# Twelve gate columns of an input projection: one split weight tile, or an fp32 product in four column groups

## The chip, the cores and the metric

The kernel runs on one core of a Trainium2 chip. The metric is the device time of one execution in microseconds. Before the change the median of three runs is 1077.58 us (1074.95 to 1078.34).

## What is computed

One inference step of a two-layer decoder, for 256 prompt tokens and 8 single-token samples, 264 columns in all, 1024 features wide. Each layer projects the normalised input with one wide matrix, feeds the pieces to four recurrent mixers (RWKV7, HGRN2, Mamba2, mLSTM), projects back, and adds cross attention over a memory and a feed-forward block:

```python
proj = rmsnorm(x, lp['norm_mix_g']) @ lp['w_in']
p_r, p_h, p_s, p_m = jnp.split(proj, GROUP_SPLITS, axis=-1)
...
x = x + mixed @ lp['w_out']
x = x + cross_attend(rmsnorm(x, lp['norm_x_g']), mem_k, mem_v, lp['xattn_wq'], lp['xattn_wo'])
hf = rmsnorm(x, lp['norm_ff_g']) @ lp['ff_w1']
x = x + jnp.square(jax.nn.relu(hf)) @ lp['ff_w2']
```

Twelve columns of `w_in` matter here. Four are Mamba2's step sizes (`dt_pre`), four the mLSTM's input gates and four its forget gates, one column per head. Everything is fp32.

## The kernel before

The activations stand transposed: `xT[k]` is feature block k (128 features) by 264 columns, k = 0 to 7. A dense product takes an fp32 weight tile `raw` of 1024 x 128 (512 KB, one DMA on SP), which ACT casts in two halves to the reduced type fp32r (`wh`, line 231) and DVE subtracts (`wl`, line 93, the rest). Its input is split in the same way, `xh` and `xl`, with the norm's gain folded in. For each of the eight blocks `dense` issues three products, wh·xh, wh·xl and wl·xh (lines 295, 296, 297), into one accumulator: 24 products a tile. The norm's factor `rstd` is multiplied in when DVE reads the accumulator. `raw` has four buffers, `wh` and `wl` three halves each.

A layer begins with eight such tiles of `w_in`, in the order 6, 2, 3, 0, 1, 4, 5, 7. The first seven are the RWKV columns. Tile 7 holds the twelve gate columns, at columns 0 to 3, 32 to 35 and 64 to 67, and zeros elsewhere; `small_rows` (line 858) turns its result `sy` into the step sizes and gates. Then three generators (RWKV, HGRN2 with mLSTM after it, Mamba2) are interleaved with the remaining `w_in` tiles and the memory's keys and values as filling work. The order of each engine's list is made by a scheduler from the order in which the program issues the work and from priorities (`later` lowers one). Each engine takes its list strictly in order.

`C(name)` is a piece of a table of constants that is loaded after the first weight tiles. Names in the rows: `LT`, `lw` are the low-rank stage of the RWKV mixer (line 410), `KV`, `qd`, `pd` with line 1365 are the cached part of the cross attention. Line 1365 issues fp32 products with 8 columns each, at accumulator partitions 0, 32, 64 and 96:

```python
for i in range(2):
    for hh in range(2):
        for a in range(2):
            b, g = b0 + a, (hh * 2 + a) * 32
            PE.matmul(ps[g:g + 8, :], lhsT=lhs[:, hh, i, b * 8:b * 8 + 8], rhs=kv[a][hh][:, i],
                      start=b < 2 and i == 0, stop=b >= NB - 2 and i == 1)
```

Of the kernel before, what the change touches and what calls it, by code (L numbers as in the profile page):

```python
# [8 lines left out]
F32 = mybir.dt.float32  # L9
# [6 lines left out]
DEPTH, DM, TP, NB, NT = 2, 1024, 256, 8, 264  # L16
KT = DM // 128
# [12 lines left out]
C_RW, C_HG, C_SS, C_ML = 0, 896, 1920, 2948  # L30


def build_consts():
    p = np.arange(128)
    cols, off, n = [], {}, 0

    def add(name, a):
        nonlocal n
        a = np.asarray(a, np.float32).reshape(128, -1)
        off[name] = (n, a.shape[1])  # L40
        n += a.shape[1]
        cols.append(a)

    add("ident", np.eye(128))
    add("blk64", (p[:, None] // 64) == (p[None] // 64))
    t64 = np.arange(64)
    s64 = (p % 64)[:, None]
    add("msi", np.concatenate([t64[None] > s64, t64[None] >= s64], 1))
    add("mh", np.stack([(p // 32) % 2 == 0, (p // 32) % 2 == 1], 1))
    t32 = np.arange(32)  # L50
    s32 = (p % 32)[:, None]
    add("id32", t32[None] == s32)
    for w in (1, 2, 4, 8, 16):
        add(f"inv{w}", ((t32[None] // w) % 2 == 1) & (s32 // w == t32[None] // w - 1))
    add("h0", t64[None] == s64)
    for w in (1, 4, 16):
        for d in (1, 2, 3):
            t = (np.arange(0, 64, 4 * w)[:, None] + np.arange(d * w, 4 * w)).reshape(-1)
            add(f"h{w}{d}", s64 // w == t[None] // w - d)
    add("mneg", np.where(p[None] >= p[:, None], 0.0, -1e30))  # L60
    add("pick", (p % 32)[:, None] == np.arange(4)[None])
    add("eye8", np.broadcast_to(np.eye(8), (128, 8, 8)))
    add("nsc", np.where(p < 32, -2.0, np.where(p < 64, 0.0, -1.0)))
    add("sgn", np.where(p >= 64, -1.0, 1.0))
    return np.ascontiguousarray(np.concatenate(cols, 1)), off
# [5 lines left out]
def body(tc, A, O, depth=DEPTH):  # L71
    nc = tc.nc
    V, S, P, PE = nc.vector, nc.scalar, nc.gpsimd, nc.tensor
# [10 lines left out]
    spool = pool("sm", 1)  # L84
# [10 lines left out]
    def mul(out, a, b):  # L95
        return tt(out, a, b, ALU.mult)
# [77 lines left out]
    xT = [xTt[:, k] for k in range(KT)]  # L174
# [1301 lines left out]
    def layer(l):  # L1476
# [34 lines left out]
            else:  # L1511
                small.append(small_rows(l, pv, ps, rstd))

        for m in (6, 2, 3, 0, 1, 4, 5, 7):
            tag = {3: "pa", 0: "pb"}.get(m, "pd") if l == 0 else "pd"
            dense([A["w_in"][l, m]], xh, xl, ev, m, ready if m == 6 else (), tag)
            if l == 0 and m == 2:
                derive(0)
            if l == 0 and m == 0:
                nc.sync.dma_start(cst, A["consts"])  # L1520
                for i in range(1, depth):
                    nc.sync.dma_start(pvt[i][:, 0:NPV], A["pv"][i])
        if l == 0 and depth > 1:
            derive(1)
        if l == 0:
# [6 lines left out]
        def proj(m0, name, order=(0, 1, 2, 3)):  # L1532
            out = [T("J", [128, 2, NT], f"{name}{i}") for i in range(4)]

            def go():
                for i in order:
                    for c in range(2):
                        dense([A["w_in"][l, m0 + 2 * i + c]], xh, xl, lambda m, ps: mul(out[i][:, m], ps, rstd), c)
                        yield
            return out, go()  # L1540

# [2 lines left out]
        def conv():  # L1544
            smp.append(tiny([128, 6, NB, 4], "smp"))
            nc.sync.dma_start(smp[0], A["conv"][l])
            for g in range(3):
                t = T("J", [128, 2, 259], "CAT")
                V.memset(t[:, :, 0:3], 0.0)

                def ev_c(m, ps, t=t):
                    mul(t[:, m, 3:259], ps[:, 0:TP], rstd[:, 0:TP])
                    mul(smp[0][:, 2 * g + m, :, 3], ps[:, TP:NT], rstd[:, TP:NT])
                for c in range(2):
                    dense([A["w_in"][l, 18 + 2 * g + c]], xh, xl, ev_c, c)
                    yield
                CAT.append(t)
            Z.append(T("J", [128, 2, NT], "Z"))
            for c in range(2):
                dense([A["w_in"][l, 16 + c]], xh, xl, lambda m, ps: mul(Z[0][:, m], ps, rstd), c)  # L1560
                yield

        PH, d_hg = proj(8, "PH", (1, 0, 2, 3))
# [143 lines left out]
def pack(x):  # L1707

    x = {k: np.asarray(v) for k, v in x.items()}
    A = {"consts": CONSTS}  # L1710
    t = np.concatenate([x["x_prompt"][0], x["x_sample"][:, 0]], 0)
    A["x"] = t.T.reshape(KT, 128, NT).transpose(1, 0, 2)
    A["mem"] = x["mem_prompt"][0].T.reshape(KT, 128, TP).transpose(1, 0, 2)

    def tiles(w):
        d, k, n = w.shape
        w = w.reshape(d, k // 1024, 8, 128, n // 128, 128).transpose(0, 4, 1, 3, 2, 5)
        return w if k > 1024 else w[:, :, 0]
    w = x["w_in"]
    sm = np.zeros((DEPTH, DM, 128), w.dtype)  # L1720
    sm[:, :, 0:4] = w[:, :, C_ML - 4:C_ML]
    sm[:, :, 32:36] = w[:, :, C_ML + 768:C_ML + 772]
    sm[:, :, 64:68] = w[:, :, C_ML + 772:C_ML + 776]
    A["w_in"] = tiles(np.concatenate([w[:, :, 0:896], sm, w[:, :, 896:C_ML - 4], w[:, :, C_ML:C_ML + 768],
                                      w[:, :, C_ML + 776:]], 2))
    for nm, k in (("wq", "xattn_wq"), ("wk", "xattn_wk"), ("ff1", "ff_w1"), ("ff2", "ff_w2")):
        A[nm] = tiles(x[k])

    w = x["xattn_wv"].reshape(DEPTH, 2, 4, 128, 4, 256).transpose(0, 4, 1, 3, 2, 5)
    A["wv"] = w.reshape(DEPTH, 4, 2, 128, 8, 128)  # L1730

    def halves(w):
        w = w.reshape(DEPTH, 2, 4, 128, 4, 2, 128).transpose(0, 1, 4, 3, 5, 2, 6)
        return w.reshape(DEPTH, 2, 4, 128, 8, 128)
    A["w_out"] = halves(x["w_out"].reshape(DEPTH, 4, 256, DM)[:, list(ORDER)])
    A["wo"] = halves(x["xattn_wo"])
    pv = np.zeros((DEPTH, 128, NPV), np.float32)
    for l in range(DEPTH):
        for nm, (o, n) in POFF.items():
            if nm in ("lb0", "lb1"):  # L1740
                v = x["hgrn_lb_logits"][int(nm[2])]
            elif nm == "final_norm_g":
                v = x[nm]
            elif nm == "D":
                v = np.repeat(x["ssm_D"][l], 64)
            elif nm in ("sbias", "alog"):
                v = np.zeros(128, np.float32)
                if nm == "sbias":
                    v[0:4], v[32:36], v[64:68] = x["ssm_dt_bias"][l], x["mlstm_i_bias"][l], x["mlstm_f_bias"][l]
                else:  # L1750
                    v[0:4] = x["ssm_A_log"][l]
            else:
                v = x[nm][l]
            pv[l, :, o:o + n] = v.reshape(n, 128).T
    A["pv"] = pv
    A["lora"] = np.concatenate([x["rwkv_w_up"], x["rwkv_a_up"], x["rwkv_g_up"]], 1)
    A["shift"] = x["state_rwkv_shift"].reshape(DEPTH, NB, 7, 128).transpose(0, 3, 2, 1)
    c = np.zeros((DEPTH, 128, 6, NB, 4), np.float32)
    c[..., 0:3] = x["state_ssm_conv"].reshape(DEPTH, NB, 3, 6, 128).transpose(0, 4, 3, 1, 2)
    A["conv"] = c  # L1760

    def quarters(s):
        return s.reshape(DEPTH, NB, 4, 4, 16, -1).transpose(0, 3, 1, 2, 4, 5).reshape(DEPTH, 128, 16, -1)
    A["wkv"], A["hgrn"] = quarters(x["state_rwkv_wkv"]), quarters(x["state_hgrn"])
    A["ssm"], A["mC"] = quarters(x["state_ssm"]), quarters(x["state_mlstm_C"])
    keyed = lambda s: s.reshape(DEPTH, NB, 2, 2, 64, 64).transpose(0, 3, 4, 2, 1, 5).reshape(DEPTH, 128, 16, 64)
    A["wkvT"], A["mCT"] = (keyed(x[k].swapaxes(3, 4)) for k in ("state_rwkv_wkv", "state_mlstm_C"))
    A["hgrnT"] = keyed(x["state_hgrn"])
    A["ssmT"] = x["state_ssm"].reshape(DEPTH, NB, 2, 2, 64, 128).transpose(0, 5, 2, 1, 3, 4).reshape(DEPTH, 128, 16, 128)
    A["mnT"] = x["state_mlstm_n"].reshape(DEPTH, NB, 2, 128).transpose(0, 3, 2, 1)  # L1770
    rep = lambda s: np.concatenate([s.reshape(DEPTH, 32, -1)] * 4, 1)
    A["mn"], A["mm"] = rep(x["state_mlstm_n"]), x["state_mlstm_m"].transpose(0, 2, 1)
    A["ck"] = x["cache_mem_k"].reshape(DEPTH, NB, 256, 4, 2, 128).transpose(0, 1, 3, 5, 4, 2)
    A["cv"] = x["cache_mem_v"].reshape(DEPTH, NB, 2, 128, 4, 256).transpose(0, 1, 4, 3, 2, 5)
    return {k: np.ascontiguousarray(v) for k, v in A.items()}
# [36 lines left out]
```

## Time and profile before

| | before |
|---|---|
| median of three runs | 1077.58 us (1074.95 to 1078.34) |
| the profiled execution | 1075.53 us |
| its span, first to last instruction | 1073.8 us |
| PE busy | 1047.8 us, 98% |
| DVE busy | 806.4 us, 75% |
| ACT busy | 630.9 us, 59% |
| mean granted TensorE clock | 0.979 |

PE is TensorE's products, PEld its weight loads, DVE VectorE, ACT ScalarE, SP the engine that issues the DMAs. Products overlap in the array, so a product's duration is longer than the distance from its start to the next start; the distance is what it takes of PE's time. An fp32 product leaves two records.

### The profile page before, as it was taken

The numbers are of one execution on the slowest core, as the hardware profiler recorded it, in microseconds if no ns is written. First come the engines' busy times: TensorE is split into PE (matmuls) and PEld (weight loads), VectorE is DVE, ScalarE is ACT, GpSimd is POOL, SyncE is SP. The second block draws the span as 40 slices with busy tenths as digits, with TensorE's granted clock in tenths as the row PEclk, the third lists the DMA queues.
The fourth block names the chain that finished last, engine by engine and source line by source line (L and its number), as shares of the span: only waits on it lengthen the run. The fifth ranks groups of instructions, "written<-read, shape, count | busy, mean of one in ns | idle before, by whom it ended". The sixth has DMA issues, their size and how long they took to land.

```text
span 1073.8 us, 26237 instructions
## 1 busy us (share of the span) xinstructions
PE 1047.8 (98%) x10334; PEld 979.0 (91%) x10334; DVE 806.4 (75%) x1846; ACT 630.9 (59%) x1352; POOL 51.7 (5%) x75
## 2 busy tenths in 40 slices
PE   8998999999999999999999999999999999999996
PEld 8997898889878999999999989888997789999996
DVE  6889785678778987755669887855886799775544
ACT  5965464467555676645569455735674466775543
POOL 2000000001001100000010000000020020000000
PEclk8999998999999999999999999989999999999999
DMA  7743456469894685555554454645978758555552
GB/s 247 235 144 102 116 150 205 149 225 329 268 361 164 232 284 183 182 178 178 186 178 158 129 142 125 192 151 167 307 251 303 277 179 293 185 177 186 180 177 80
DMA packets 81579, 213.44 MB, mean 199 GB/s; under 512 B 16432, under 2 KB 19120, under 8 KB 81456
## 3 DMA queue, kind: packets, MB, share of 16 engines
q1 hardware_dynamic: 81456, 211.77, 61.0%
q8 instruction: 81, 1.33, 0.5%
q14 instruction: 42, 0.34, 0.1%
HBM read 195.86 MB, written 15.87 MB: 197 GB/s over the span
## 4 chain that ended last, share of the span: by engine, by line
PE 90%; DVE 6%; ACT 1%; DMA 1%; issue 0%; POOL 0%; SPq 0%; DVEq 0%; ACTq 0%
PE pd L295 20%; PE pd L297 20%; PE pd L296 20%; PE pm L1365 3%; PE pd L308 3%; PE pd L309 2%; PE pd L310 2%; PE pd L1318 1%; PE pd L1319 1%; PE pm L1427 1%; PE pd L1320 1%; DVE wl L93 1%; PE pm L1452 1%; PE pm L345 1%; PE pm L150 1%; PE pm L941 1%
## 5 line engine op out<-in xcount | busy, mean ns | idle before, releaser
L231 ACT CAST wh<-raw 128x512 fp32r<-128x512 f32 x544 | 335.5, 619 | 281.2 <-PE pd L296 228.6
L93 DVE TENSOR_TENSOR wl<-raw,wh 128x512 fp32r<-128x512 f32 x544 | 378.2, 699 | 153.8 <-ACT wh L231 142.6
L295 PE MATMUL pd<-xh,wh 128*128 128x264 f32 x1136 | 332.1, 292 | 0.4 <-ACT wh L231 0.4
L297 PE MATMUL pd<-xh,wl 128*128 128x264 f32 x1136 | 328.4, 289 | 2.9 <-DVE wl L93 2.9
L296 PE MATMUL pd<-xl,wh 128*128 128x264 f32 x1136 | 327.1, 288 | 2.4 <-DVE xl L111 2.4
L295 PEld LDWEIGHTS pd<-xh,wh 128*128 128x128 f32 x1136 | 217.1, 191 | 7.1 <-issue 2.8
L297 PEld LDWEIGHTS pd<-xh,wl 128*128 128x128 f32 x1136 | 217.8, 192 | 5.3 <-DVE wl L93 4.5
L296 PEld LDWEIGHTS pd<-xl,wh 128*128 128x128 f32 x1136 | 217.1, 191 | 3.3 <-DVE xl L111 3.0
L295 PE MATMUL pd<-hid,wh 128*128 128x264 f32 x512 | 146.0, 285 | 0.0
L297 PE MATMUL pd<-hid,wl 128*128 128x264 f32 x512 | 145.7, 285 | 0.0
L296 PE MATMUL pd<-hid,wh 128*128 128x264 f32 x512 | 145.5, 284 | 0.0
L296 PEld LDWEIGHTS pd<-hid,wh 128*128 128x128 f32 x512 | 96.6, 189 | 0.0
L297 PEld LDWEIGHTS pd<-hid,wl 128*128 128x128 f32 x512 | 96.4, 188 | 0.0
L295 PEld LDWEIGHTS pd<-hid,wh 128*128 128x128 f32 x512 | 96.3, 188 | 0.0
L108 POOL TENSOR_TENSOR nacc<-nacc,nsq 128x264 f32<-128x264 f32 x41 | 39.2, 955 | 958.6 <-ACT nsq L90 698.1
L93 DVE TENSOR_TENSOR xT<-xT,pd 128x264 f32<-128x264 f32 x80 | 34.0, 425 | 16.2 <-PE pd L310 8.9
L295 PE MATMUL pd<-mgh,wh 128*128 128x256 f32 x128 | 39.7, 310 | 0.0
L308 PE MATMUL pd<-oh,wh 128*128 128x264 f32 x128 | 37.7, 297 | 1.9 <-DVE xT L93 1.9
L297 PE MATMUL pd<-mgh,wl 128*128 128x256 f32 x128 | 38.7, 302 | 0.0
L296 PE MATMUL pd<-mgl,wh 128*128 128x256 f32 x128 | 38.0, 297 | 0.0
L310 PE MATMUL pd<-oh,wl 128*128 128x264 f32 x128 | 36.6, 287 | 0.5 <-DVE wl L93 0.5
L309 PE MATMUL pd<-ml,wh 128*128 128x264 f32 x128 | 36.5, 285 | 0.0
(559 smaller groups left out, 1828.8 us busy)
## 6 DMA issues: line engine op xcount, KB each, us to landing
raw<-in_ff SPq DMA_DIRECT2D x128, 512.0 KB, 3.7
raw<-in_w_in SPq DMA_DIRECT2D x63, 512.0 KB, 3.6
KV<-in_ck SPq DMA_DIRECT2D x64, 256.0 KB, 5.1
KV<-in_cv SPq DMA_DIRECT2D x64, 256.0 KB, 5.6
raw<-in_wk SPq DMA_DIRECT2D x16, 512.0 KB, 4.8
raw<-in_wv SPq DMA_DIRECT2D x16, 512.0 KB, 3.7
raw<-in_w_out SPq DMA_DIRECT2D x16, 512.0 KB, 4.7
raw<-in_wq SPq DMA_DIRECT2D x16, 512.0 KB, 4.4
```

The costliest lines, as they stand in the source:

```text
L93: return V.tensor_tensor(out, a, b, op=op)
L108: return P.tensor_tensor(out, a, b, op=ALU.add)
L150: PE.matmul(ps, lhsT=blk64, rhs=src[:, j], start=True, stop=True)
L231: S.copy(h, src)
L295: PE.matmul(ps, lhsT=wh, rhs=x, start=i * 8 + k == 0, stop=False)
L296: PE.matmul(ps, lhsT=wh, rhs=y, start=False, stop=False)
L297: PE.matmul(ps, lhsT=wl, rhs=x, start=False, stop=i * 8 + k == n - 1)
L308: PE.matmul(ps, lhsT=wh, rhs=h[k], start=k == 0, stop=False)
L309: PE.matmul(ps, lhsT=wh, rhs=lo[k], start=False, stop=False)
L310: PE.matmul(ps, lhsT=wl, rhs=h[k], start=False, stop=k == 3)
L345: PE.matmul(ps[hs, j, b], lhsT=St[hs, j * 8 + b, :], rhs=cols(hs, j, b), start=True, stop=True)
L1365: PE.matmul(ps[g:g + 8, :], lhsT=lhs[:, hh, i, b * 8:b * 8 + 8], rhs=kv[a][hh][:, i], start=b < 2 and i == 0, stop=b >= NB - 2 and i == 1)
```

## The change

The gate columns leave the wide matrix. They become a weight of their own, `wg`, 1024 x 32 (twelve columns used), 128 KB a layer, in one buffer. It isn't split: DVE multiplies the norm's gain into it, and eight fp32 products take it against the unnormalised `xT[k]`. Product k writes accumulator partitions 32 (k mod 4) to 32 (k mod 4) + 31, so each group of 32 partitions sums two blocks. ACT copies that accumulator to `gpart`, and one more fp32 product with a constant 0/1 matrix `gsum` sums the four groups and puts the rows where `small_rows` expects them.

```diff
+    gate = np.where(p % 32 < 12, p % 32 // 4 * 32 + p % 4, -1)
+    add("gsum", gate[:, None] == p[None])
...
-        for m in (6, 2, 3, 0, 1, 4, 5, 7):
+        wg = spool.tile([128, 8, 32], F32, tag="wg", name="wg", bufs=1)
+
+        def gates():
+            mul(wg, wg, pv["norm_mix_g"][:, :, None].to_broadcast([128, 8, 32]))
+            ps = psum("pb", [128, NT], "pg")
+            for k in range(KT):
+                g = k % 4 * 32
+                PE.matmul(ps[g:g + 32], lhsT=wg[:, k], rhs=xT[k], start=k < 4, stop=k >= 4)
+            part = SB.s1([128, NT], "gpart")
+            S.copy(part, ps)
+            ps = psum("pb", [128, NT], "pg")
+            PE.matmul(ps, lhsT=C("gsum"), rhs=part, start=True, stop=True)
+            ev(7, ps)
+
+        for m in (6, 2, 3, 0, 1, 4, 5):
             tag = {3: "pa", 0: "pb"}.get(m, "pd") if l == 0 else "pd"
             dense([A["w_in"][l, m]], xh, xl, ev, m, ready if m == 6 else (), tag)
...
+            if m == 0:
+                nc.sync.dma_start(wg, A["wg"][l])
+        gates()
...
-    sm = np.zeros((DEPTH, DM, 128), w.dtype)
+    sm = np.zeros((DEPTH, DM, 32), w.dtype)
     sm[:, :, 0:4] = w[:, :, C_ML - 4:C_ML]
-    sm[:, :, 32:36] = w[:, :, C_ML + 768:C_ML + 772]
-    sm[:, :, 64:68] = w[:, :, C_ML + 772:C_ML + 776]
-    A["w_in"] = tiles(np.concatenate([w[:, :, 0:896], sm, w[:, :, 896:C_ML - 4], w[:, :, C_ML:C_ML + 768],
+    sm[:, :, 4:12] = w[:, :, C_ML + 768:C_ML + 776]
+    A["wg"] = sm.reshape(DEPTH, KT, 128, 32).transpose(0, 2, 1, 3)
+    A["w_in"] = tiles(np.concatenate([w[:, :, 0:896], w[:, :, 896:C_ML - 4], w[:, :, C_ML:C_ML + 768],
                                       w[:, :, C_ML + 776:]], 2))
```

The other edits only lower the index of the later `w_in` tiles by one.

The scheduler moves work with it. On PE in the first layer, before, the end of the gates' dense tile (the last three of its 24 products), then two low-rank products, then the next projection:

```order
L295 MATMUL pd<-xh,wh 128x264
L296 MATMUL pd<-xl,wh 128x264
L297 MATMUL pd<-xh,wl 128x264
L410 MATMUL pm<-LT,lw 128x264 x2
L295 MATMUL pd<-xh,wh 128x264
```

And with the change, from the end of the dense tile of m = 5 (lines are two higher; `pg` is the gates' accumulator):

```order
L297 MATMUL pd<-xh,wh 128x264
L298 MATMUL pd<-xl,wh 128x264
L299 MATMUL pd<-xh,wl 128x264
L1523 MATMUL pg<-xT,wg 32x264 x8
L412 MATMUL pm<-LT,lw 128x264 x2
L1527 MATMUL pg<-gpart,cst 128x264
L297 MATMUL pd<-xh,wh 128x264
```

The 24 products of the gates' tile are gone; eight grouped products, the same two low-rank products and the sum stand between two dense tiles. The second layer has the same rows.

On ACT at that place, with the change (`raw_585` is the next projection's first tile, `raw_637` its second):

```order
L233 CAST wh_587<-raw_585 128x512
L92 ACTIVATE t1_672<-PR2_178,pv0_77 128x264
L233 CAST wh_591<-raw_585 128x512
L233 CAST wh_639<-raw_637 128x512
L1525 COPY gpart_448<-pg_439 128x264
L92 ACTIVATE sw_565<-pm_568,pv0_77 128x264
```

The copy to `gpart` stands behind three half-tile casts; the third takes the buffer that the last half of m = 5 leaves.

On DVE in the first layer, further on, with the change (`ssp`, `sy` are the gates' results, `PH0` a projection, `wg_7875` the second layer's gate weights):

```order
L1086 COPY lli_2049<-sy_452 4x264
L95 TENSOR_TENSOR PH0_535<-pd_682,rstd_173 128x264
L95 TENSOR_TENSOR lmr_2007<-lmr_2007,llf_2048 4x8
L1145 MEMSET RL_2219 128x256
L95 TENSOR_TENSOR wl_769<-raw_766,wh_768 128x512
L95 TENSOR_TENSOR lmr_2007<-lmr_2007,lli_2049 4x8
L95 TENSOR_TENSOR wg_7875<-wg_7875,pv1_78 128x256
```

Before, `lli`, the `lmr` rows and the fill of `RL` stand some 185 places later on DVE, behind most of the HGRN2 chunk work; now they are in the middle of the projections, with the second layer's scaling of `wg` behind them.

## Rows read from the trace of the kernel before

**Rows 1.** The page's head: span, busy time, and the chain that ended last

```profile
span 1073.8 us, 26237 instructions
...
PE 1047.8 (98%) x10334; PEld 979.0 (91%) x10334; DVE 806.4 (75%) x1846; ACT 630.9 (59%) x1352; POOL 51.7 (5%) x75
...
PE 90%; DVE 6%; ACT 1%; DMA 1%; issue 0%; POOL 0%; SPq 0%; DVEq 0%; ACTq 0%
```

**Rows 2.** Stretches: length, busy PE PEld DVE ACT POOL, PE clock, DMA share, GB/s

```profile
40.00:50.00 10.00, 10.00 (x76) 9.03 (x75) 10.00 (x27) 10.00 (x24) 0.00 (x0) 1.00 0.64 183
...
70.00:80.00 10.00, 10.00 (x133) 9.23 (x132) 6.70 (x18) 3.46 (x8) 0.00 (x0) 0.83 0.24 62
...
90.00:100.00 10.00, 6.61 (x90) 6.10 (x94) 10.00 (x49) 6.22 (x17) 0.00 (x0) 0.96 0.16 57
...
620.00:630.00 10.00, 7.92 (x116) 6.92 (x116) 10.00 (x52) 6.12 (x17) 0.00 (x0) 1.00 0.44 148
```

**Rows 3.** Timeline of PE, first products of two tiles: start, duration in us, work

```profile
21.84 0.29 PE L295 MATMUL pb<-xh,wh 128*128 128x264 f32 x1
...
24.77 0.29 PE L295 MATMUL pd<-xh,wh 128*128 128x264 f32 x1
```

**Rows 4.** Timeline of PE around two low-rank products

```profile
36.38 0.28 PE L297 MATMUL pd<-xh,wl 128*128 128x264 f32 x1
36.59 0.71 PE L410 MATMUL pm<-LT,lw 32*128 32x264 f32 x4
37.24 0.39 PE L295 MATMUL pd<-xh,wh 128*128 128x264 f32 x1
37.47 0.28 PE L296 MATMUL pd<-xl,wh 128*128 128x264 f32 x1
```

**Rows 5.** Timeline of PE around eight grouped fp32 products of the attention

```profile
295.08 0.28 PE L297 MATMUL pd<-xh,wl 128*128 128x264 f32 x1
295.29 1.05 PE L1365 MATMUL pm<-KV,pd 128*8 128x256 f32 x16
296.27 0.39 PE L295 MATMUL pd<-xh,wh 128*128 128x264 f32 x1
```

**Rows 6.** Timeline of PE around one full fp32 product

```profile
17.98 0.60 PE L264 MATMUL pc<-nacc,ones 128*128 128x264 f32 x2
...
18.54 0.28 PE L295 MATMUL pd<-xh,wh 128*128 128x264 f32 x1
```

**Rows 7.** Timeline of ACT: reading an fp32 product's result, and a copy of this shape

```profile
18.68 0.48 ACT L90 ACTIVATE rstd<-pc,epst 128x264 f32<-128x264 f32 x1 [1.31 <-PE pc L264]
...
45.80 0.37 ACT L425 COPY gg<-pm 128x264 f32<-128x264 f32 x1
```

**Rows 8.** DVE: timeline of two subtractions; groups: operations, count, busy us, mean ns

```profile
13.20 1.28 DVE L93 TENSOR_TENSOR wl<-raw,wh 128x512 fp32r<-128x512 f32 x2
...
L93 DVE TENSOR_TENSOR macc<-macc,msq 128x256 f32<-128x256 f32 x14 | 5.9, 420 | 1.7 <-ACT msq L90 1.6
...
L1084 DVE COPY lli<-sy 4x264 f32<-4x264 f32 x1 | 0.3, 284 | 0.0
...
L93 DVE TENSOR_TENSOR lmr<-lmr,llf 4x8 f32<-4x8 f32 x1 | 0.2, 155 | 0.0
```

**Rows 9.** Line 1365: weight loads, duration ns min/median/max, first and last start

```profile
L1365 PEld LDWEIGHTS pm<-KV,pd x256: 85/90/90, 295.3 to 853.6; 128*8 128x8 f32 x128
```

**Rows 10.** Timeline of PE at one-column products; stretches as in rows 2

```profile
71.89 2.03 PE L345 MATMUL pm<-hfq,SHT__1038 64*64 64x1 f32 x64
...
75.00:78.50 3.50, 3.50 (x20) 3.26 (x20) 1.50 (x4) 1.22 (x4) 0.00 (x0) 0.55 0.17 22
...
280.50:284.00 3.50, 3.50 (x41) 1.73 (x40) 3.20 (x12) 1.56 (x6) 0.00 (x0) 1.00 0.69 200
```

**Rows 11.** DMA: issues on SP's timeline; sizes with median us to landing

```profile
11.07 11.10 SPq L277 DMA_DIRECT2D raw<-in_w_in  x4
...
raw<-in_w_in SPq DMA_DIRECT2D x63, 512.0 KB, 3.6
```

More of the change, by code (lines that the diff above doesn't have):

```diff
@@ L1537, in go @@
                     for c in range(2):
-                        dense([A["w_in"][l, m0 + 2 * i + c]], xh, xl, lambda m, ps: mul(out[i][:, m], ps, rstd), c)
+                        dense([A["w_in"][l, m0 - 1 + 2 * i + c]], xh, xl, lambda m, ps: mul(out[i][:, m], ps, rstd), c)
                         yield
@@ L1554, in conv @@
                 for c in range(2):
-                    dense([A["w_in"][l, 18 + 2 * g + c]], xh, xl, ev_c, c)
+                    dense([A["w_in"][l, 17 + 2 * g + c]], xh, xl, ev_c, c)
                     yield
@@ L1559, in conv @@
             for c in range(2):
-                dense([A["w_in"][l, 16 + c]], xh, xl, lambda m, ps: mul(Z[0][:, m], ps, rstd), c)
+                dense([A["w_in"][l, 15 + c]], xh, xl, lambda m, ps: mul(Z[0][:, m], ps, rstd), c)
                 yield
```

## The prediction

> **What bounds the kernel now.** The first view to read is the page's head: PE counts as busy for 1047.8 of 1073.8 us, and the chain that ended last runs through PE for 90% and through DVE for 6% [rows 1]. So work taken off PE should be worth nearly its full length, unless DVE decides at that place. The second view shows where it does: table by stretch, both mixer stages [rows 2]. At 40 to 50 us PE and DVE are both full. At 70 to 80 us DVE has 3.3 us to spare. At 90 to 100 us (and at 620 to 630 us in the second layer) DVE is full and PE is not, with 3.4 and 2.1 us idle: there DVE's list of work is the bound. The third view is the timeline of PE around the places that the change touches; each price below is read there from starts, not from durations, since neighbouring products overlap.
>
> **What goes from PE.** Per layer one dense tile, 24 products. The first product of one tile starts at 21.84 us, of the next at 24.77 us [rows 3]: 2.93 us, or 0.122 us a product. With it go, per layer, two casts on ACT, two subtractions on DVE (0.64 us each [rows 8]) and a load of 512 KB.
>
> **What comes to PE.** Eight fp32 products of 32 columns each, in four column groups, then one full fp32 product that sums the groups.
>
> 1. The eight grouped products. The kernel has this form already, in the cached part of the attention: 8 columns, 256 moving columns, four groups. There 16 records (each fp32 product leaves two) start at 295.29 us and the next work starts at 296.27 us: 0.98 us for eight products [rows 5]. A full-width fp32 product of 264 columns, taken alone, moves the next start by 18.54 - 0.122 - 17.98 = 0.44 us [rows 6], so eight in single file would be 3.52 us. The four groups thus do run side by side. The moving side grows from 256 to 264 columns: 0.98 x 264/256 = 1.01 us. The new weights are 32 columns wide instead of 8. The weight loads of the narrow form take 85 to 90 ns [rows 9] beside the passes, and I take 1.01 us. Switching into a grouped form costs 0.09 us (295.29 against 295.08 + 0.122).
>
> 2. The order puts two products of the low-rank stage behind the eight, which stood alone between dense tiles before: from 36.38 us to the next steady start they cost 37.47 - 0.122 - 36.38 - 0.122 = 0.85 us, 0.20 us of it for switching in and out [rows 4]. Behind the eight they need 0.65 us (start to next start).
>
> 3. The sum product is full width: 0.44 us, and the 0.11 us of switching back.
>
> 4. The sum waits for the copy. A reader on ACT started 0.10 us after the fp32 product ended (17.98 + 0.60, then 18.68), and a copy of this shape takes 0.37 us [rows 7]. From the first grouped product: about 1.08 us to the end of the last, 0.10, 0.37, and some 0.10 us back, so the sum may start at 1.65 us; PE arrives there at 1.01 + 0.65 = 1.66 us. I take no wait, with a bound of 0.6 us, one cast on ACT ahead of the copy.
>
> Per layer: before 2.93 + 0.85 = 3.78 us; after 0.09 + 1.01 + 0.65 + 0.44 + 0.11 = 2.30 us. **PE gains 1.5 us a layer.**
>
> **What DVE and ACT do with it.** In the second layer DVE loses two subtractions (1.2 us) ahead of its full stretch and gets nothing, because the scaling of that layer's gate weights is placed in the first layer: the 1.5 us stand. In the first layer DVE loses 1.2 us, and gets two scalings (128 x 256, 0.42 us each by the operation of that shape [rows 8]). The new order also pulls the mLSTM's small row operations ahead of its full stretch: a copy of 0.28 us, a fill of the same length and five of at most 0.16 us [rows 8], some 1.3 us. DVE so has about 0.9 us more to do before 80 us, with 3.3 us free at 70 to 80 us. If that takes it up, the first layer gains 1.5 us too; if it doesn't, because DVE is already full when the extra work comes, PE waits for it and loses up to 0.9 us. I take 0.8 us, nearer to the upper end, since the free time lies between this work and the stretch that decides.
>
> **Other edits.** The new order breaks the dense stream three more times behind this place, over both layers; by the 0.20 us of switching that is 0.6 us. The constants grow by 64 KB and the gate weights bring 128 KB ahead of the fifth weight tile. By the time to landing of a 512 KB tile, 3.6 us, 192 KB are at most 1.4 us of transfer; the loads behind it are issued only from 11.07 us on, four of them over 11.1 us, each when a buffer comes free [rows 11]: they wait for buffers, not for the transfer. I take 0, and at worst 1.4 us. The second layer's load of gate weights waits on SP until the first layer's products have read the one buffer; it stands behind loads for the mixers, which are issued after that place anyway: 0.
>
> **Sum.** -0.8 - 1.5 + 0.6 = -1.7 us. The profiled execution took 1075.53 us in all, 1.7 us of it outside the span and untouched, so one like it should take 1073.8 us. It lies 2.05 us below the median of the three runs, 1077.58 us. Against that median: **1075.9 us**, 0.16% less. A measurement of this kernel can tell about 0.3%, 3.2 us, from no change: faster means below 1074.3, slower above 1080.8 us.
>
> **A rule against the change.** The attention's rows show four column groups running at once with all 128 rows in each [rows 5]. The Trainium skill, "TensorE: Matmul & The Clock Gate", section "What overlaps and what doesn't", states that weight loads run beside products in flight only when the row group differs. By that rule none of these loads would overlap, since every product here uses all rows, and the sum would be that of the second rival. The trace disagrees for 8 columns; for 32 no row exists.
>
> **Rivals.**
>
> *More is gained.* Clock is given back. After 64 records of one-column products PE's granted clock was 0.55 in the stretch from 75 to 78.5 us, nearly all of it at the lower of its two levels, 1.2 instead of 2.4 GHz [rows 10]. That costs 3.5 x 0.45 = 1.6 us. Both the place and the timing of such stretches change with the order behind the gates. For it: they sit right behind work that moves. Against it: the same products are still there. With one or two fewer: 1075.9 - 1.6 to - 3.2, that is 1074.3 to 1072.7 us; with DVE's spare time taking everything up, 0.7 us less still.
>
> *The groups go in single file (slower).* The place is the eight products; the price is a pass of 0.22 us (half of 0.44) instead of one of about 0.06. Then they take 3.52 us, 2.5 us more per layer, and both layers lose: -1.7 + 5.0 = +3.3, 1080.9 us. If the weight loads (at least 85 ns, sixteen a layer, 1.4 us) don't hide either: +6.0, 1083.6 us. It decides from the length of a pass: the gain is gone at 1.01 + 0.85 = 1.86 us for the eight, 116 ns a pass. Against it speak the 61 ns a pass of the attention's rows; for it, that the weights are four times as wide here.
>
> *A clock stretch is added.* The grouped products, the narrow ones and a wait stand together for some 2.3 us. In the attention such a stretch kept the full clock, 1.00 at 280.5 to 284 us [rows 10], which speaks against it. At 1.6 us for one or two: 1077.5 to 1079.1 us, no change.
>
> *The sum waits on ACT.* The copy stands behind a cast that can start only when PE has left the last dense tile. If it is late, each layer loses up to 0.6 us: 1077.1 us, no change. That the tile is not really taken away can be excluded: the order has 24 dense products fewer per layer.
>
> **How the numbers follow.** Forecast, 0.50: its own range by the bounds above (at best 1.5 us in both layers and nothing for the breaks, -3.0; at worst +0.9 - 1.5 + 0.6 = 0) is 1074.6 to 1077.6 us. More gained 0.24; single file 0.07; added clock stretch 0.12; sum waits 0.07. Faster by over 0.3% are the second case and, since the three runs shown spread over 3.4 us themselves, the edge of the first, 0.30. Slower by over 0.3% are single file and a tail where several clock stretches meet, 0.10. The rest, 0.60, is no change. The range leaves out single file's upper part and the tail of the large gains: 1071.9 to 1080.0 us.
>
> **What would show it.** Right: sixteen records of the gate products within 1.0 to 1.1 us, a sum that starts less than 0.2 us after the low-rank products, and the first product of the next projection about 1.5 us earlier in each layer than before. The first layer's full stretch of DVE at 90 to 100 us should move ahead by about 0.8 us. Wrong: records of the gates 0.2 us apart, an idle row before the sum released by the copy on ACT, waits of PE on DVE at 70 to 80 us, where it has none now [rows 2], or a granted clock near a half in stretches that are at full clock now.

## The result, and the profile after

| | before | after |
|---|---|---|
| median | 1077.24 us (1074.95 to 1078.34, 6 runs) | 1083.32 us (1081.91 to 1085.83, 6 runs) |
| the profiled execution | 1075.53 us | 1084.26 us |
| mean granted clock | 0.979 | 0.972 |

The ratio is 1.0054, interval 1.0037 to 1.0070: the change costs about 6 us. The page's head of the changed kernel, to be held against [rows 1]:

```profile
span 1082.4 us, 26205 instructions
...
PE 1052.5 (97%) x10322; PEld 980.7 (91%) x10322; DVE 804.5 (74%) x1844; ACT 629.4 (58%) x1350; POOL 51.3 (5%) x75
```

PE has less work (twelve records fewer) and is busy 4.7 us longer. Timeline of PE at the gates in the first layer (line 1523 is the eight grouped products, 412 the low-rank pair, 1527 the sum):

```profile
32.83 0.28 PE L299 MATMUL pd<-xh,wl 128*128 128x264 f32 x1
33.05 1.10 PE L1523 MATMUL pg<-xT,wg 128*32 128x264 f32 x16
34.08 0.71 PE L412 MATMUL pm<-LT,lw 32*128 32x264 f32 x4
34.72 0.71 PE L1527 MATMUL pg<-gpart,cst 128*128 128x264 f32 x2
35.08 0.48 PE L297 MATMUL pd<-xh,wh 128*128 128x264 f32 x1
35.40 0.28 PE L298 MATMUL pd<-xl,wh 128*128 128x264 f32 x1
```

The weight loads of line 1523 (durations in ns, min/median/max):

```profile
L1523 PEld LDWEIGHTS pg<-xT,wg x32: 106/109/111, 33.0 to 568.3; 128*32 128x32 f32 x32
```

ACT's timeline at the copy that the sum waits for:

```profile
34.21 0.38 ACT L1525 COPY gpart<-pg 128x264 f32<-128x264 f32 x1 [0.52 <-PE pg L1523]
```

Here all went as priced. The eight take 34.08 - 33.05 = 1.03 us, the pair 0.64, and from the end of the dense stream (32.83 + 0.122) to its next steady product (35.40 - 0.122) it is 2.33 us, where the sum of the prediction has 2.30. So the loss arises behind the gates. The table by stretch, with the rows that answer to [rows 2] and two more:

```profile
40.00:50.00 10.00, 10.00 (x76) 9.30 (x75) 9.05 (x25) 10.00 (x24) 0.00 (x0) 1.00 0.55 172
50.00:60.00 10.00, 9.16 (x72) 8.82 (x71) 9.37 (x25) 9.78 (x23) 0.00 (x0) 1.00 0.51 162
60.00:70.00 10.00, 9.30 (x109) 8.70 (x107) 7.33 (x21) 7.23 (x22) 0.00 (x0) 0.84 0.51 166
70.00:80.00 10.00, 9.52 (x118) 8.77 (x118) 6.96 (x18) 2.70 (x6) 0.00 (x0) 0.84 0.17 50
90.00:100.00 10.00, 8.41 (x118) 7.34 (x116) 9.99 (x43) 6.82 (x19) 0.00 (x0) 1.00 0.47 155
...
620.00:630.00 10.00, 9.11 (x132) 8.58 (x132) 10.00 (x41) 4.83 (x12) 0.00 (x0) 1.00 0.47 160
```

Two stretches of the kernel before, for comparison:

```profile
50.00:60.00 10.00, 10.00 (x76) 9.38 (x75) 9.96 (x25) 9.77 (x24) 0.00 (x0) 1.00 0.53 180
60.00:70.00 10.00, 10.00 (x128) 9.76 (x127) 8.47 (x24) 7.98 (x22) 0.00 (x0) 1.00 0.63 200
```

At 40 to 50 us ACT is full, as before, but DVE is a tenth less busy. From 50 us on PE waits (it was at 10.00 in the three stretches from 50 to 80 us before), and at 60 to 70 us the clock falls, where it was 1.00. The same two things happen in the second layer, where executions agree best. Four moments count there: DVE reads the last RWKV tile (`PR`, the reference point, just ahead of the gates), PE starts the thin products on RWKV's states (two columns each, `rRV`, the first state product) and on HGRN2's (one column, `hfq`, the second), and DVE reads the last Mamba2 tile (`Z`). Timelines of the kernel before, then of the changed one:

```profile
563.00 0.43 DVE L93 TENSOR_TENSOR PR<-pd,rstd 128x264 f32<-128x264 f32 x1 [0.18 <-PE pd L297]
593.57 2.03 PE L345 MATMUL pm<-rRV,SWT 64*64 64x2 f32 x64
599.83 1.21 PE L345 MATMUL pm<-hfq,SHT__8728 64*64 64x1 f32 x36
672.12 0.40 DVE L93 TENSOR_TENSOR Z<-pd,rstd 128x264 f32<-128x264 f32 x1
```

```profile
567.89 0.43 DVE L95 TENSOR_TENSOR PR<-pd,rstd 128x264 f32<-128x264 f32 x1 [0.18 <-PE pd L299]
597.56 2.19 PE L347 MATMUL pm<-rRV,SWT 64*64 64x2 f32 x64
607.69 2.09 PE L347 MATMUL pm<-hfq,SHT__8690 64*64 64x1 f32 x64
680.79 0.40 DVE L95 TENSOR_TENSOR Z<-pd,rstd 128x264 f32<-128x264 f32 x1
```

From the reference point: first state product 30.57 us before, 29.67 after; second 36.83 and 39.80; `Z` 109.12 and 112.90. So 0.9 us of what the gates saved is still there at the first; 3.9 us are lost from there to the second. What changed ahead of them stands on ACT. Two of RWKV's chains pass through it: `kk` (from the key) with `nrm`, and `cp` (the decays, which DVE's scans prepare). ACT's timeline before:

```profile
574.82 0.93 ACT L90 ACTIVATE kk<-k,pv 128x264 f32<-128x264 f32 x2
576.15 0.65 ACT L90 ACTIVATE nrm<-kk 128x528 f32<-128x528 f32 x1
...
583.04 0.64 ACT L90 ACTIVATE cp<-cp 128x512 f32<-128x512 f32 x1
```

and after, from one cast of a weight half-tile to the next:

```profile
583.35 0.60 ACT L233 CAST wh<-raw 128x512 fp32r<-128x512 f32 x1
583.86 0.37 ACT L427 COPY gg<-pm 128x264 f32<-128x264 f32 x1
584.13 0.52 ACT L92 ACTIVATE kk<-k,pv 128x264 f32<-128x264 f32 x1
584.55 0.36 ACT L427 COPY gg<-pm 128x264 f32<-128x264 f32 x1
584.81 0.52 ACT L92 ACTIVATE kk<-k,pv 128x264 f32<-128x264 f32 x1
585.23 0.63 ACT L92 ACTIVATE hsg<-PH 128x528 f32<-128x528 f32 x1
585.76 0.63 ACT L92 ACTIVATE nrm<-kk 128x528 f32<-128x528 f32 x1
586.29 0.61 ACT L233 CAST wh<-raw 128x512 fp32r<-128x512 f32 x1
...
595.22 0.63 ACT L92 ACTIVATE cp<-cp 128x512 f32<-128x512 f32 x1 [1.01 <-DVE cp L95]
```

From the reference point `kk` starts at 11.8 us before and 16.2 after, `cp` at 20.0 and 27.3. In the changed kernel both copies of `gg` and all of `kk` stand in a lump between two casts, 2.9 us apart. DVE, which subtracts what was cast, stands still for it. Its timeline after:

```profile
584.59 0.42 DVE L450 TENSOR_TENSOR_SCAN cc<-ones,sw 128x128 f32<-128x128 f32 x1
586.93 0.69 DVE L95 TENSOR_TENSOR wl<-raw,wh 128x512 fp32r<-128x512 f32 x1 [1.92 <-ACT wh L233]
```

The 2 us in which ACT works on `kk`, before and then after; DVE is the third engine in the row:

```profile
574.00:576.00 2.00, 2.00 (x16) 1.77 (x15) 1.97 (x5) 2.00 (x6) 0.00 (x0) 1.00 0.05 8
```

```profile
584.00:586.00 2.00, 2.00 (x18) 2.00 (x17) 1.01 (x2) 2.00 (x6) 0.00 (x0) 1.00 1.74 33
```

Behind `kk`, in both layers, PE waits for ACT and DVE; before it waited for neither from 50 to 80 us and from 590 to 615 us. PE's rows with a wait in brackets, changed kernel:

```profile
53.29 0.49 PE L152 MATMUL pm<-nrm,cst 128*128 128x264 f32 x1 [0.84 <-ACT nrm L92]
...
61.25 0.39 PE L299 MATMUL pd<-xh,wl 128*128 128x264 f32 x1 [0.70 <-DVE wl L95]
...
596.00 0.39 PE L299 MATMUL pd<-xh,wl 128*128 128x264 f32 x1 [0.32 <-DVE wl L95]
...
605.93 0.36 PE L297 MATMUL pd<-xh,wh 128*128 128x264 f32 x1 [0.65 <-ACT wh L233]
```

And right behind both state products of the second layer the granted clock is 0.50, its lower level (1.00 throughout 594 to 604 us before):

```profile
600.00:602.00 2.00, 2.00 (x9) 1.80 (x8) 1.62 (x6) 1.80 (x5) 0.00 (x0) 0.50 0.58 170
...
610.00:612.00 2.00, 2.00 (x10) 1.95 (x10) 0.52 (x2) 0.00 (x0) 0.00 (x0) 0.50 0.04 4
```

Summed over the span in windows of 2 us, each counted as 2 us times what its granted clock lacks of 1, the clock takes 24.0 us before and 30.9 after, in portions of 1.7 us: four more. This isn't one profile's chance alone. The mean granted clock is on record for every run; span times what it lacks of 1 is 28.7 us on average in the six runs of the changed kernel and 21.3 in the twenty of the kernel before that ran beside e1. So 7 us more go to the clock, and the rest of the span is 1 us shorter.

### The profile page after: what moved, and what is told of

Its sections match the earlier page's. It is cut to its first block, busy times and chain, and to the rows that moved or that the text cites. A ratio compares the mean times of both kernels' runs of the same rounds, so it can differ in the third digit from the quotient of the medians.

```text
span 1082.4 us, 26205 instructions
## 1 busy us (share of the span) xinstructions
PE 1052.5 (97%) x10322; PEld 980.7 (91%) x10322; DVE 804.5 (74%) x1844; ACT 629.4 (58%) x1350; POOL 51.3 (5%) x75
## 5 line engine op out<-in xcount | busy, mean ns | idle before, releaser
L310 PE MATMUL pd<-mh,wh 128*128 128x264 f32 x128 | 36.5, 285 | 0.0
```

Of the source, the lines that this page charges most:

```text
L310: PE.matmul(ps, lhsT=wh, rhs=h[k], start=k == 0, stop=False)
```

## Theories and experiments

Three theories. **S**, supply: what PE saves becomes waits on ACT and DVE, and these bring half-clock stretches, whatever the order. **P**, product: the gates' pieces cost the time themselves. **O**, order: the lists that the scheduler made hold RWKV's `kk` and `gg` (the low-rank pair of line 426) too late; put back in place, the loss goes. The lists say how far apart the cases are; dense products issued in a layer ahead of each piece on PE:

| | `gg`, one and two | state products, first and second |
|---|---|---|
| before | 50 and 96 behind the first low-rank pair | 384, 408 |
| after | 96, as a pair | 360 (362 in the second layer), 388 |

Medians and ratios to the kernel before, run beside each (the kernel before had medians of 1076.82 to 1078.88 us in these sittings):

| run | us | ratio, interval |
|---|---|---|
| e1_drop | 1071.38 | 0.9945 (0.9922 to 0.9969) |
| e2_dead24 | 1084.98 | 1.0079 (1.0056 to 1.0101) |
| e5_gg | 1076.95 | 0.9998 (0.9979 to 1.0016) |
| e4_l1 | 1081.52 | 1.0041 (1.0021 to 1.0061) |
| e3_l0 | 1079.71 | 1.0014 (0.9998 to 1.0029) |
| e6_hold | 1082.35 | 1.0046 (1.0023 to 1.0069) |
| e7_kkfirst | 1073.16 | 0.9960 (0.9936 to 0.9985) |
| e10_kkfirst | 1074.24 | 0.9969 (0.9948 to 0.9989) |
| e8_early | 1073.37 | 0.9957 (0.9936 to 0.9977) |
| e9_b_early | 1076.97 | 0.9989 (0.9970 to 1.0008) |

### e1_drop: no gates at all

```diff
-        gates()
...
-            else:
+            if m == 5:
                 small.append(small_rows(l, pv, ps, rstd))
```

> The gate columns are not projected at all: neither the dense tile nor the grouped products and their sum; the gates read the accumulator of the dense tile m=5 instead, so this kernel leaves out that part of the computation. PE has 24 x 0.122 = 2.93 us less than before in each layer and nothing in exchange. Its lists have the RWKV copies gg apart again, as before the change. Theory S (supply and clock: what PE saves in front of the one-column state products it waits for on ACT and DVE, and those waits bring stretches of half clock, 1.7 us each): no gain of that size, 1076 to 1084 us, waits of PE on wl or wh between 50 and 64 us and more half-clock stretches than the ten of before. Theory P (the grouped products, their sum or the gain multiplied on DVE cost it): they are gone, so 1077.2 - 5.9 = 1071.4 us, 1069 to 1073. Theory O (the new order on ACT, with the RWKV copies late): order as before, so 1071 to 1074 us.

Measured 1071.38 us, 5.4 below before. S falls: 5.9 us taken off PE are worth 5.4 here, so ACT and DVE do not stand in the way by themselves; nor do the runs lose more to the clock (20.6 us on average, against 21.3). P and O are both left, since with the gates' pieces gone the early `gg` came back too.

### e2_dead24: more work on PE

```diff
         gates()
+        ps = psum("pd", [128, NT], "pd")
+        for i in range(24):
+            PE.matmul(ps, lhsT=xh[i % 8][:, 0:128], rhs=xh[(i + 1) % 8], start=i == 0, stop=i == 23)
```

> The changed kernel with 24 dead products of 128x264 per layer behind the gates, where the dense tile stood: no load, no cast, nobody reads them. PE has 5.9 us more to do than in the changed kernel. Theory S: the waits ahead of the state products go, and with them the four added half-clock stretches (4 x 1.7 = 6.8 us); time 1077 to 1082 us, less than the changed kernel in spite of the added work. Theories P and O: the added products cost their length, 1083.3 + 5.9 = 1089 us (1087 to 1091).

Measured 1084.98 us, between the two ranges: neither was met. The profiled execution took 1085.02 us with 25.8 us lost to the clock; less the clock that is 1059.2, against 1084.26 - 30.9 = 1053.4 of the changed kernel: the dead products cost 5.8 us, their whole length, and the clock took 5.1 us less. The clocks of all runs say much the same: 24.4 us lost in these four and 28.7 in the changed kernel's six, 5.9 us more elsewhere. So more work on PE does take off some half-clock time, as S has it, but less than it costs. It doesn't bring back what the late chain costs: in the second layer `kk` starts at 19.3 us, and both half-clock stretches stayed.

### e5_gg: one product earlier

```diff
+        for j in (0,):
+            ps = pst([128, NT])
+            PE.matmul(ps, lhsT=lw[64:128, j * 128:(j + 1) * 128], rhs=LT[64:128], start=True, stop=True)
+            S.copy(gg[:, j], ps)
         nc.sync.dma_start(O["o_shift"][l], sho)
...
-        for j in range(2):
+        for j in (1,):
```

> The changed kernel with the first of the two low-rank gate products of RWKV (gg, with its copy on ACT) issued one step earlier in the program; on ACT gg and kk then stand two casts earlier, about where they stood before the change. Theory O (RWKV's chain is late because gg and kk stand late on ACT): most of the loss goes, 1077 to 1080 us. Theories S and P: no change beyond what a moved wait or one half-clock stretch makes, 1081 to 1086 us.

Measured 1076.95 us: the whole loss is gone, by issuing one product and its copy a step earlier, with the gates as they are. P falls and O stands. What the gates gain on PE doesn't show yet; `kk` starts 13.4 us from the reference point here, later than before (11.8). In the second layer the first state product comes at 29.11 us from the reference point, the second at 35.40, `Z` at 108.07.

### e4_l1 and e3_l0: one layer each

```diff
-        for m in (6, 2, 3, 0, 1, 4, 5):
+        for m in (6, 2, 3, 0, 1, 4, 5) + (() if l == 1 else (7,)):
...
-        gates()
+        if l == 1:
+            gates()
```

(and 0 in place of 1 in e3_l0.)

> The new gates in the second layer alone; the first keeps its dense tile. In the changed kernel the delay against before grew by 4.9 us up to the end of the first layer's mixers and by 3.7 us in the second's. All theories that place the cost in each layer by itself: 1077.2 + 3.7 = 1081 us (1079.5 to 1082.5), with no added half-clock stretch before 540 us and two more in 590 to 620 us (S). If the first layer's delay causes the second's: within 1 us of before, or below it by the 1.5 us that the gates save on PE, 1075.5 to 1078 us.

> The new gates in the first layer alone; the second keeps its dense tile. In the lists the first layer's gg products are a late pair and its second state product stands at 388 dense products, as in the changed kernel; the second layer's stand apart and its state products come 24 products apart, as before. Theory O: the second layer as before (first state product 30.6 us and Z 109 to 112 us behind the last RWKV tile's evacuation); the first layer loses what is left of the changed kernel's loss after the second layer's (e4_l1: 1081.5 us, 4.4 above before): 1077.6 + 1.5 = 1079 us, 1077 to 1081.5. If the first layer alone carries the loss: 1082 to 1084 us.

Measured 1081.52 and 1079.71 us, 4.7 and 2.1 above before; together 6.8, where the change cost 6.1. The 2.1 alone are not clear of noise, since the interval includes 1. In e3_l0 the second layer is the old one to a few hundredths of a microsecond (30.57, 36.83, `Z` 109.08). The part of the first expectation on the clock missed: the profiled execution of e4_l1 has three more half-clock stretches in the first layer too, whose order is that of before. One profile can't weigh them; the section at the end comes back to this.

### e6_hold: the kernel before, with the late order

```diff
+        hold = tiny([128, 1], "hold")
+        P.tensor_tensor(hold[64:128], a[64:128, 1, 263:264], a[64:128, 1, 263:264], op=ALU.subtract)
+        P.tensor_tensor(LT[64:128, 0:1], LT[64:128, 0:1], hold[64:128], op=ALU.add)
```

> The kernel before the change, gates and all, with one thing added: two operations on POOL (64 x 1 each) that give the low-rank gate's input a value unchanged but only once a is finished. In the lists the two gg products then stand as a pair and kk with its chain stands four casts later on ACT, as in the changed kernel, in both layers; the state products move from 384 and 408 dense products into the layer to 386 and 412. Theory O (the late gg and kk cost the time): slower than before by the loss of the changed kernel without its gain on PE, 1080 to 1086 us, with half-clock stretches behind both state products of the second layer. Theory S (PE's saving turns into waits): nothing is saved here, so no loss, 1075.5 to 1078.5 us.

Measured 1082.35 us, slower than before by 0.23 to 0.69%, without any part of the change. The second layer, as above:

```profile
564.43 0.43 DVE L93 TENSOR_TENSOR PR<-pd,rstd 128x264 f32<-128x264 f32 x1 [0.18 <-PE pd L297]
595.84 2.03 PE L345 MATMUL pm<-rRV,SWT 64*64 64x2 f32 x64
606.20 2.03 PE L345 MATMUL pm<-hfq,SHT__8734 64*64 64x1 f32 x64
678.58 0.40 DVE L93 TENSOR_TENSOR Z<-pd,rstd 128x264 f32<-128x264 f32 x1
```

The second state product is 41.77 us from the reference point, 4.9 later than before, and 10.4 behind the first, as in the changed kernel (10.1). The clock fell behind both. `kk` starts at 18.2 us, `cp` at 29.1. This is O from the other side. But the late order costs only 3.5 us here, where the changed kernel is some 10 us slower than e8 below, which has it early; why it weighs more there is open.

### e7_kkfirst, e10_kkfirst: only the chain is moved

```diff
+        kk, nrm, k2 = s2("kk"), s2("nrm"), s2("k2")
+        for j in range(2):
+            act(kk[:, j], k[:, j], AF.Copy, scale=pv["rwkv_k_k"][:, j:j + 1])
+        act(nrm, kk, AF.Square)
         for j in range(2):
             ps = pst([128, NT])
```

(the four lines are taken away behind the `gg` loop.)

> The changed kernel with kk and the first step of nrm issued ahead of the two gg products. In ACT's list kk then stands seven casts earlier than in the changed kernel, nrm five, while the gg products stay a pair. If it is kk's chain that must not be late: as e5, 1074 to 1078 us. If it is the gg product or copy itself: 1081 to 1085 us.

> e7 again, with more rounds: 1072 to 1075 us, below the kernel before by 0.2 to 0.6%, if e7's result was no chance of where the half-clock stretches fell; within 0.2% of before if it was.

Measured 1073.16 and 1074.24 us, both below the kernel before. The `gg` products are still a late pair here, so it is `kk`'s chain that must not be late; in the lists of before, after and e5 `kk` follows the first `gg`. In the second layer `kk` starts at 4.6 us, earlier than before the change too (11.8), and `cp`, which was not moved, at 22.5 instead of 27.3.

### e8_early and e9_b_early: with the order in hand, what are the gates worth?

`kk`, the first step of `nrm` and both `gg` products move ahead of the store of `o_shift`, in the changed kernel (e8) and in the kernel before (e9).

> The changed kernel with kk, the first step of nrm and both gg products issued one step earlier in the program. In the lists kk stands seven casts earlier on ACT than in the changed kernel, gg two, and the state products stand at 360 and 384 dense products into the layer, which is where the kernel before has them less the 24 of the removed tile. Theory O: the loss goes and the gain that was priced for the gates on PE shows, 2.9 us: 1072 to 1076 us, at or below e7. Without theory O: 1081 to 1085 us.

> The kernel before the change (dense gate tile) with the same early issue of kk, nrm and gg as e8. Its state products stay at 384 and 408. If the early issue itself makes e8 fast: as fast as e8, within 1 us. If it only keeps RWKV's chain in its place, and the gates save PE time: before's time, 1076 to 1079 us, and e8 is 2 to 4 us faster than this.

Measured 1073.37 and 1076.97 us: e9 is as fast as the kernel before, though `kk` starts at 8.4 us instead of 11.8, and e8 beats both kernels. So an earlier `kk` alone gains nothing, and the gates save 3.6 us by the medians, 2.8 by the means, where PE's rows gave 2.9. With runs that spread over some 7 us this agrees. Second layer of e8:

```profile
562.35 0.43 DVE L95 TENSOR_TENSOR PR<-pd,rstd 128x264 f32<-128x264 f32 x1 [0.18 <-PE pd L299]
591.08 2.03 PE L347 MATMUL pm<-rRV,SWT 64*64 64x2 f32 x64
598.94 0.40 PE L347 MATMUL pm<-hfq,SHT__8690 64*64 64x1 f32 x8
...
671.27 0.40 DVE L95 TENSOR_TENSOR Z<-pd,rstd 128x264 f32<-128x264 f32 x1
```

The first state product comes at 28.73 us, 1.84 ahead of before. Against it the late order of the changed kernel costs 0.94 us up to there. From there to `Z` it is 78.55 us before (no stretch of half clock behind either product), 80.19 in e8 (one), 83.23 after (two, 3.4 us, the wait of 0.65, and 0.6 not traced further). -1.84 + 0.94 + 4.68 = +3.78 us, the second layer's share.

### r_before and r_after: the two kernels again

> The kernel before, a second profile. If the half-clock stretches follow from the order: ten of 1.7 us between 20 and 1060 us again and 24 us lost in all (22.3 to 25.7), none between 590 and 615 us. If they are chance: another number and other places.

> The changed kernel itself, a second profile. If the four added half-clock stretches follow from its order: about 30.9 us lost to the clock again (29 to 33), with stretches right behind both state products of the second layer. If they are chance from execution to execution: another number, 24 to 29 us, and other places.

r_before took 1081.24 us, 5.7 more than the profile shown, with 24.3 us lost to the clock, 0.3 more; but the stretches lie elsewhere (among them 124 to 130, 158 to 164 and 598 to 604 us). Most of the 5.7 us is idle time of PE, 30.9 us of the span instead of 26.0; 2.5 of it is one wait, at line 568, for which the profile shows no releaser. r_after took 1082.14 us, 27.5 lost, again with a stretch behind both state products of the second layer. So where the stretches fall is partly chance. So is their number: the 29 runs of the kernel before beside e8 have granted clocks from 0.975 to 0.986, which is 27 to 15 us lost. Those two places are not chance alone: behind the second state product of the second layer the clock fell in all five profiles with the late order there (after twice, e2, e4, e6) and in two of nine with the early one (e1, e10); behind the first in four of five, and in three of nine.

## Why the prediction was wrong

The range ended at 1080.0 us and slower had a chance of 0.10; it came to 1083.32.

- **What goes from PE, what comes to PE**: right. 2.93 us for the tile (e1: 5.4 us for both), 1.03 for the eight, 0.64 for the pair, no wait for the copy, 2.33 us in all for 2.30. With the order held, e8 against e9 is 3.6 us (2.8 by the means) for a predicted 3.0 over both layers.
- **The rule against the change**: the trace disagrees for 32 columns too. By "TensorE: Matmul & The Clock Gate" of the Trainium skill, "What overlaps and what doesn't", a weight load overlaps only if its row group differs; here sixteen loads of 106 to 111 ns, all on 128 rows, add up to 1.7 us and lie within 1.03 us of products.
- **Other edits** is the step that failed. It read the new order on PE, found three more breaks of the dense stream and priced them at 0.6 us. The new order on ACT and DVE cost about 9 us: -3.0 for the gates, +6 measured. Against e8, which has the gates and the early order, it is 9.9: 6.2 us go to the clock and 3.7 elsewhere (averages over the runs). `gg` on PE and `kk` on ACT were not looked for, and the one row that shows `gg`'s copy [rows 7] was read only for its length.
- **What DVE and ACT do with it** failed by the same omission. It counted how much work DVE gets and looked for free time (3.3 us at 70 to 80 us). The bound was at 40 to 60 us. Of the row at 40 to 50 us the prediction took PE and DVE as full and passed over ACT, which is at 10.00 too [rows 2] (and at 9.78 of 10 from 50 us on after). What a full engine takes first decides there: `kk` starts 5.8 us later than before from the first layer's reference point, 4.4 us in the second's, DVE is idle first (1.01 busy of 2.00), and PE waits afterwards.
- **A clock stretch is added**, the rival with 0.12, had the mechanism, at 1.6 us each (1.7 measured), but not the place (behind the state products, not at the gates) nor the number: one or two were priced, and the profile has four (7 us on average over the runs). Its other bound, that the clock stays at 1.00, holds at the gates.
- **Single file** and **the sum waits on ACT** are refuted by the rows of lines 1523 and 1525.
- Of what would show it wrong, two came: waits of PE on DVE, though at 61 us and not at 70 to 80, and a granted clock near a half where it was full.

What isn't shown is why the scheduler's order turned. It is not the missing tile, since e1 has the early `gg` without it; it comes with the gates' pieces, in each layer that has them. Nor is it shown why the late chain brings half-clock stretches behind the state products.

## What to carry to other kernels

Where a scheduler orders the lists, compare the new lists on every full engine, not only on the one that gets or loses work, and look for the first step of each long chain: its place there may be worth more than the edit. If a small local gain comes out as a loss, hold that chain in place in the old and in the new kernel: the pair (here e8 and e9) gives the edit's own worth, and the order's. Here that turned +6 us into -4.

## What the hardware showed

The clock falls to its lower level in portions that cost 1.7 us each, and two executions of one kernel have them at other places: the two profiles of the kernel before lose 24.0 and 24.3 us. From the reference point to the first state product, where none falls, the same two agree within 0.02 us (30.57 and 30.55 in the second layer), and so do those of the changed kernel (29.67 and 29.69). So a landmark ahead of the first such stretch measures an edit of 1 us in one profile, which medians of runs that spread over nearly 10 us (1071.94 to 1081.52 for the kernel before in one sitting) barely do.

The Trainium skill, "TensorE: Matmul & The Clock Gate", section "HAM oscillation — how this bites in real kernels", puts such falls down to waits of PE. In the kernel before PE has no idle time from 70 to 80 us [rows 2], and the clock falls there behind sixty-four one-column products [rows 10], so it took no wait. Nor do such products decide alone: in the same profile the granted clock stays at 1.00 behind both state products of the second layer.
